# Token-major products of a hybrid decoder layer: alternating the two token tiles

## The chip, the cores and the metric

The kernel runs on one core of a Trainium2 chip. The metric is the device time of one execution in microseconds (us), lower is better. A run is an execution of the whole layer, weights read from device memory included.

## What is computed

One layer of a hybrid decoder trunk for 256 tokens and 2048 channels, all in fp32. Cut to its products:

```python
h = rms_norm(x, norm_mix_pre)
p = h @ w_in                                  # projections of three token mixers, and gate_raw
y_a, y_b, y_c = rglru(...), gated_deltanet(...), rwkv7(...)     # 1024 channels each
m = sum(sigmoid(gate_raw[b]) * (y_b @ w_branch[b]) for b in range(3))
x = x + rms_norm(m @ w_out, norm_mix_post)
h = rms_norm(x, norm_ffn_pre)
x = x + rms_norm((silu(h @ w_gate) * (h @ w_up)) @ w_down, norm_ffn_post)   # 5632 wide
```

The mixers are a gated linear recurrence, a chunked delta rule and a generalised delta rule. Nothing in the change touches their arithmetic.

## The kernel before

**Split operands.** Every large product is made from split fp32 numbers. An activation `x` is held as a high part `xh` (rounded to the type fp32r) and a low part `xl = x - xh`; a weight tile likewise as `wh` and `wl`. The product is the sum of three TensorE matmuls: `xh` with `wh` ("hi hi"), `xh` with `wl` ("hi lo"), and `xl` with `wh` ("lo hi"); the low-by-low one is left out.

**Two layouts.** `block_b` (lines 228 to 246) makes channel-major products: the weights are the stationary operand, 256 tokens move through (lines 241 to 243), into one PSUM bank. It serves the mixers' inputs. `block_a_steps` (lines 253 to 278) makes token-major products: 128 tokens of the activation are the stationary operand and 512 weight columns move through. Since there are 256 tokens, a block has two token tiles, t = 0 and t = 1, and each has an accumulator of its own, `ps[0]` and `ps[1]`, a whole PSUM bank each. The blocks are: 12 of the gates (`w_mix`, 16 channel tiles k each), 12 of the branches (`w_branch`, 8 each), 4 of `w_out` (16 each), 11 of `w_gate` and 11 of `w_up` (16 each) and 4 of `w_down` (44 each). That makes 12 x 16 + 12 x 8 + 4 x 16 + 22 x 16 + 4 x 44 = 880 steps of k, each of six matmuls: 5280.

**The change's place.** For each k, `products(t, k, h, l)` issues the three matmuls of one token tile: line 262 is hi hi, line 263 is hi lo, line 264 is lo hi. The loop calls it for tile 0 and then for tile 1:

```python
for k, h, l in self.weights(wp, src, kts, 512):
    mm = products(0, k, h, l)
    kept.append((k, h, l))
    if not last or k < kts - LATE:
        for a in kept:
            products(1, *a)
        kept = []
```

With `last` (the fourth block of `w_out` and of `w_down`) the tile 1 products of the last `LATE` = 6 steps of k are kept back and issued after all of tile 0, so that tile 0 can be emptied meanwhile.

**Weights.** `weights` (lines 190 to 218) loads 1 MB at a time into `raw` by a DMA on the queue of SyncE (SP, line 203). ScalarE (ACT) rounds 1024 columns to `wh` (line 214, three buffers), VectorE (DVE) subtracts to get `wl` (line 216, three buffers). With 512 columns one such pair serves two steps of k, which is twelve matmuls.

**Emptying.** A block's `sink` reads `ps[0]` and `ps[1]` when they are complete: the gates by ACT at line 980, the branches by DVE at lines 1058 to 1062, `w_gate` by ACT at line 1150, `w_up` by DVE at line 1154. While the mixers run, every block takes its two accumulators from a set of three banks (tag "mm"), so one of them is still being emptied when the next block begins; later, blocks take turns between two sets of three (`self.turn`).

**What sets the order.** The kernel is written with a framework that orders the instructions of each engine itself: it takes them in program order with priorities, and lets an instruction go ahead of an earlier one whose operands or buffers are, by its own model, not yet ready. So PE's order is not that of the source: a tile's first product may come later than written where its bank is not yet free, and hi lo may come later where `wl` is not yet there. Small fp32 matmuls of the mixers (and transposes, line 285) stand between the large ones, in the same queue.

**Other lines.** Line 642 and 649 (DVE) make the last result `yt` of a mixer quarter, line 650 stores it to DRAM `y` on SP's queue; line 1039 reads `y` back as `yf` for a branch, and line 1049 a kept gate. FFN block j = 0 interleaves the steps of `w_gate` and `w_up`, four of each at a time.

Of the kernel before, what the change touches and what calls it, by code (L numbers as in the profile page):

```python
# [14 lines left out]
P = 128  # L15
T = 256
D = 2048
KD = D // P
# [6 lines left out]
LATE = 6  # L25
# [115 lines left out]
class Builder:  # L141
# [108 lines left out]
        for _ in self.block_a_steps(wp, pp, src, xh, xl, kts, sink, last):  # L250
            pass

    def block_a_steps(self, wp, pp, src, xh, xl, kts, sink, last=False):
        nc = self.nc
        self.turn = 1 - getattr(self, "turn", 0)
        tag, n = ("mm", self.mm_bufs) if self.turn or self.mixers else ("ptg", self.ps_bufs["ptg"])
        ps = [pp.tile([P, 512], F32, name=self.uid("mm"), tag=tag, bufs=n) for _ in range(2)]
        kept = []

        def products(t, k, h, l):  # L260
            ts = slice(t * P, (t + 1) * P)
            nc.tensor.matmul(ps[t], xh[:, k, ts], h, start=(k == 0), stop=False)  # L262
            nc.tensor.matmul(ps[t], xh[:, k, ts], l, start=False, stop=False)  # L263
            return nc.tensor.matmul(ps[t], xl[:, k, ts], h, start=False, stop=(k == kts - 1))  # L264

        for k, h, l in self.weights(wp, src, kts, 512):
            mm = products(0, k, h, l)
            kept.append((k, h, l))
            if not last or k < kts - LATE:
                for a in kept:  # L270
                    products(1, *a)
                kept = []
            yield k
        with self.tc.issue_after(mm.ins):
            for a in kept:
                products(1, *a)
        with self.tc.high_priority(self.ahead_evac):
            sink(ps)

# [598 lines left out]
def build(tc, aps, out):  # L878
    nc = tc.nc
    b = Builder(tc)  # L880
# [5 lines left out]
    pp = b.pp = b.pool("pp", space=bass.MemoryType.PSUM)  # L886
    b.dp = b.pool("dram", space=bass.MemoryType.DRAM)
    cp = b.pool("const")
    wp = b.pool("wp")
# [3 lines left out]
    def acts(s):  # L893
        return (xp.tile([P, KD, T], F32R, name=f"{s}h", tag="xh"), xp.tile([P, KD, T], F32R, name=f"{s}l", tag="xl"))
# [6 lines left out]
    xh, xl = acts("x")  # L901
# [82 lines left out]
    def stage(s):  # L984
        return sp.tile([P, 512], F32, name=b.uid(s), tag="stage", bufs=b.stage_bufs)
# [133 lines left out]
    xh, xl = acts("h")  # L1119
    with tc.high_priority(FIRST):  # L1120
# [5 lines left out]
        last = b.to_channels(pp, group, "n3", xh, xl)  # L1126
# [18 lines left out]
    for j in range(FF // 512):  # L1145
        g = [stage("silu") for _ in range(2)]

        def gate(ps, g=g):
            for t in range(2):
                nc.scalar.activation(g[t], ps[t], AF.Silu, scale=rs[t])  # L1150

        def up(ps, g=g):
            for t in range(2):
                nc.vector.scalar_tensor_tensor(g[t], ps[t], rs[t], g[t], ALU.mult, ALU.mult)

        steps = [b.block_a_steps(wp, pp, aps[w][j], xh, xl, KD, f) for w, f in (("w_gate", gate), ("w_up", up))]
        if j == 0:
            for _ in range(0, KD, 4):
                for st in steps:
                    for _ in range(4):  # L1160
                        next(st)
        for st in steps:
            for _ in st:
                pass
        b.hold = None
        for t in range(2):
            b.split_channels(pp, g[t], ah, al, 4 * j, t)
# [49 lines left out]
```

## Time and profile before

| | |
|---|---|
| median of 3 runs | 1847.26 us (1846.95 to 1848.06) |
| the profiled execution's own time | 1846.92 us |
| its span, first to last instruction | 1845.1 us |
| PE (TensorE matmul) busy | 1827.5 us, 99% |
| PEld (weight load) busy | 1578.7 us, 86% |
| DVE busy | 1123.7 us, 61% |
| ACT busy | 863.8 us, 47% |
| mean granted TensorE clock | 0.996 of full speed |
| share of the chain that ended last | PE 96%, DVE 1%, ACT 1%, DMA 1% |

A matmul's duration in the trace runs from its start to its modelled end, and successive ones overlap; how fast the engine goes is read from the distance of their starts. In a name such as `mm<-wh,hl` the first operand is the moving one and the second the stationary one, so `wh,hl` is a weight's high part moving past an activation's low part: lo hi. Buffer numbers are left out there; which of the two accumulators a row writes is seen from the order of instructions below. `h`, `m`, `x`, `y` and `a` ahead of `h` or `l` stand for the activation: layer input `x`, mixer outputs `y`, merged `m`, FFN input `h`, FFN middle `a`.

### The profile page before, as it was taken

What the parts mean: (1) busy time and instruction counts of PE and PEld (TensorE: products, weight loads), DVE (VectorE), ACT (ScalarE), POOL (GpSimd) and SP (SyncE); (2) the same over time, 40 slices, a digit from 0 to 9 for tenths busy, and PEclk for the clock granted to TensorE, in tenths of its full rate; (3) what the DMA queues carried; (4) which work ended last, traced back from release to release, by engine and by line L of the source; (5) the groups of instructions that cost most, each with busy time, mean ns of one, the idle gap of its engine ahead of it and who ended that gap; (6) DMA issues with size and microseconds to landing.
All of it is one profiled execution on the core that took longest, in us unless ns stands there. A gap on an engine that the chain in (4) does not pass through costs nothing.

```text
span 1845.1 us, 27756 instructions
## 1 busy us (share of the span) xinstructions
PE 1827.5 (99%) x11516; PEld 1578.7 (86%) x11516; DVE 1123.7 (61%) x1652; ACT 863.8 (47%) x1089; POOL 41.0 (2%) x76
## 2 busy tenths in 40 slices
PE   9999999999999999999999999999999999999998
PEld 9999997999899988887788878888888888888886
DVE  6768567866786677746665556555545445444444
ACT  7545345534553465444444446444444444443443
POOL 0000000000100010000000000000000000000000
PEclk9999999999999999999999999999999999999999
DMA  7545445444544454657765556555555555555553
GB/s 263 176 168 183 146 148 189 168 159 138 183 170 159 144 181 161 221 179 271 279 218 185 186 202 231 197 187 185 195 191 183 187 196 187 207 203 185 202 185 136
DMA packets 58574, 347.45 MB, mean 188 GB/s; under 512 B 6480, under 2 KB 7760, under 8 KB 19920
## 3 DMA queue, kind: packets, MB, share of 16 engines
q1 hardware_dynamic: 50832, 328.23, 50.8%
q10 hardware_dynamic: 7328, 15.36, 2.3%
q8 instruction: 90, 1.47, 0.3%
q0 software_dynamic: 288, 2.10, 0.3%
q14 instruction: 36, 0.29, 0.0%
HBM read 330.98 MB, written 14.68 MB: 187 GB/s over the span
## 4 chain that ended last, share of the span: by engine, by line
PE 96%; DVE 1%; ACT 1%; DMA 1%; issue 0%; POOL 0%; ACTq 0%; POOLq 0%; DVEq 0%; SPq 0%
PE mm L263 21%; PE mm L264 21%; PE mm L262 21%; PE mm L242 8%; PE mm L241 8%; PE mm L243 8%; PE tp L285 1%; PE px L568 1%; PE pr L603 1%; PE pr L592 1%; PE psa L599 1%; DMA raw<-in_w_branch_dram 1%; PE pst L609 0%; PE px L753 0%; PE px L482 0%
## 5 line engine op out<-in xcount | busy, mean ns | idle before, releaser
L216 DVE TENSOR_TENSOR wl<-raw,wh 128x1024 fp32r<-128x1024 f32 x590 | 721.4, 1224 | 607.0 <-ACT wh L214 604.4
L214 ACT CAST wh<-raw 128x1024 fp32r<-128x1024 f32 x590 | 620.5, 1052 | 839.3 <-PE mm L264 601.8
L242 PE MATMUL mm<-xl,wh 128*128 128x256 f32 x1200 | 342.5, 286 | 1.6 <-DVE xl L915 1.5
L241 PE MATMUL mm<-xh,wh 128*128 128x256 f32 x1200 | 342.8, 286 | 0.1
L243 PE MATMUL mm<-xh,wl 128*128 128x256 f32 x1200 | 341.4, 285 | 0.0
L264 PE MATMUL mm<-wh,hl 128*128 128x512 f32 x704 | 274.7, 390 | 0.0
L263 PE MATMUL mm<-wl,hh 128*128 128x512 f32 x704 | 274.6, 390 | 0.0
L262 PE MATMUL mm<-wh,hh 128*128 128x512 f32 x704 | 250.9, 392 | 2.0 <-ACT hh L311 2.0
L242 PEld LDWEIGHTS mm<-xl,wh 128*128 128x128 f32 x1200 | 229.8, 191 | 3.6 <-DVE xl L915 2.2
L241 PEld LDWEIGHTS mm<-xh,wh 128*128 128x128 f32 x1200 | 229.8, 191 | 1.9 <-ACT xh L914 0.5
L243 PEld LDWEIGHTS mm<-xh,wl 128*128 128x128 f32 x1200 | 229.5, 191 | 0.9 <-issue 0.3
L262 PEld LDWEIGHTS mm<-wh,hh 128*128 128x128 f32 x704 | 132.4, 188 | 29.6 <-ACT hh L311 2.6
L263 PEld LDWEIGHTS mm<-wl,hh 128*128 128x128 f32 x704 | 132.5, 188 | 27.6 <-DVE wl L216 0.4
L264 PEld LDWEIGHTS mm<-wh,hl 128*128 128x128 f32 x704 | 132.4, 188 | 27.5
L263 PE MATMUL mm<-wl,xh 128*128 128x512 f32 x384 | 151.7, 395 | 0.3 <-DVE wl L216 0.3
L264 PE MATMUL mm<-wh,xl 128*128 128x512 f32 x384 | 150.6, 392 | 0.0
L262 PE MATMUL mm<-wh,xh 128*128 128x512 f32 x384 | 141.3, 392 | 0.0
L264 PE MATMUL mm<-wh,al 128*128 128x512 f32 x352 | 136.9, 389 | 0.0
L263 PE MATMUL mm<-wl,ah 128*128 128x512 f32 x352 | 136.9, 389 | 0.0
L262 PE MATMUL mm<-wh,ah 128*128 128x512 f32 x352 | 123.6, 389 | 0.0
L263 PEld LDWEIGHTS mm<-wl,xh 128*128 128x128 f32 x384 | 72.1, 188 | 16.9 <-issue 1.0
L262 PEld LDWEIGHTS mm<-wh,xh 128*128 128x128 f32 x384 | 72.1, 188 | 16.0 <-issue 1.3
(297 smaller groups left out, 1951.4 us busy)
## 6 DMA issues: line engine op xcount, KB each, us to landing
raw<-in_w_in_dram SPq DMA_DIRECT2D x72, 1024.0 KB, 4.9
raw<-in_w_mix_dram SPq DMA_DIRECT2D x48, 1024.0 KB, 5.0
raw<-in_w_gate_dram SPq DMA_DIRECT2D x44, 1024.0 KB, 4.8
raw<-in_w_up_dram SPq DMA_DIRECT2D x44, 1024.0 KB, 4.9
raw<-in_w_down_dram SPq DMA_DIRECT2D x44, 1024.0 KB, 4.9
raw<-in_w_branch_dram SPq DMA_DIRECT2D x24, 1024.0 KB, 4.9
raw<-in_w_out_dram SPq DMA_DIRECT2D x16, 1024.0 KB, 4.8
keep<-stage ACTq DMA_DIRECT2D x28, 256.0 KB, 4.4
```

Of the source, the lines that this page charges most:

```text
L214: nc.scalar.copy(wh[:, :n], s)
L216: nc.vector.tensor_tensor(wl[:, :n], s, wh[:, :n].bitcast(F32), ALU.subtract)
L241: nc.tensor.matmul(o, hs, xh[:, k], start=(k == 0 and c == 0), stop=False, skip_group_check=True)
L242: nc.tensor.matmul(o, hs, xl[:, k], start=False, stop=False, skip_group_check=True)
L243: nc.tensor.matmul(o, ls, xh[:, k], start=False, stop=(k == kts - 1), skip_group_check=True)
L262: nc.tensor.matmul(ps[t], xh[:, k, ts], h, start=(k == 0), stop=False)
L263: nc.tensor.matmul(ps[t], xh[:, k, ts], l, start=False, stop=False)
L264: return nc.tensor.matmul(ps[t], xl[:, k, ts], h, start=False, stop=(k == kts - 1))
L285: nc.tensor.transpose(ps[:, k], src[:, k * P:(k + 1) * P], self.cst("id"))
L568: nc.tensor.matmul(ps[h][:, n * P:(n + 1) * P], bkc[hs, c, n], arc[hs, c, n], start=True, stop=True)
L592: nc.tensor.matmul(pq[bb, us], st[u][:, n, bb], sav[:, n, us], start=not n, stop=True, skip_group_check=True)
L599: nc.tensor.matmul(ps[bb, us], X[bb, 2 * u + p], R[bb, us], start=True, stop=True)
```

## The change

`products` now takes a list of token tiles. For each of the three kinds (hi hi, hi lo, lo hi) it issues that kind for every tile of the list, so that with both tiles listed each matmul adds to the other bank than the one before it. The order of the three kinds within a tile is the same as before. FFN block j = 0 passes `paired=False`, which keeps the old order tile by tile, and the kept-back steps of a `last` block are still issued one tile after the other. Matmuls, weight loads, loads, casts and evictions are the same in number and size.

```diff
--- before.py
+++ after.py
@@ -250,30 +250,31 @@
         for _ in self.block_a_steps(wp, pp, src, xh, xl, kts, sink, last):
             pass
 
-    def block_a_steps(self, wp, pp, src, xh, xl, kts, sink, last=False):
+    def block_a_steps(self, wp, pp, src, xh, xl, kts, sink, last=False, paired=True):
         nc = self.nc
         self.turn = 1 - getattr(self, "turn", 0)
         tag, n = ("mm", self.mm_bufs) if self.turn or self.mixers else ("ptg", self.ps_bufs["ptg"])
         ps = [pp.tile([P, 512], F32, name=self.uid("mm"), tag=tag, bufs=n) for _ in range(2)]
         kept = []
 
-        def products(t, k, h, l):
-            ts = slice(t * P, (t + 1) * P)
-            nc.tensor.matmul(ps[t], xh[:, k, ts], h, start=(k == 0), stop=False)
-            nc.tensor.matmul(ps[t], xh[:, k, ts], l, start=False, stop=False)
-            return nc.tensor.matmul(ps[t], xl[:, k, ts], h, start=False, stop=(k == kts - 1))
+        def products(ts, k, h, l):
+            for a, w, first, end in ((xh, h, True, False), (xh, l, False, False), (xl, h, False, True)):
+                for t in ts:
+                    mm = nc.tensor.matmul(ps[t], a[:, k, t * P:(t + 1) * P], w, start=first and k == 0,
+                                          stop=end and k == kts - 1)
+            return mm
 
         for k, h, l in self.weights(wp, src, kts, 512):
-            mm = products(0, k, h, l)
-            kept.append((k, h, l))
-            if not last or k < kts - LATE:
-                for a in kept:
-                    products(1, *a)
-                kept = []
+            if last and k >= kts - LATE:
+                mm = products((0,), k, h, l)
+                kept.append((k, h, l))
+            else:
+                for ts in ((0, 1),) if paired else ((0,), (1,)):
+                    mm = products(ts, k, h, l)
             yield k
         with self.tc.issue_after(mm.ins):
             for a in kept:
-                products(1, *a)
+                products((1,), *a)
         with self.tc.high_priority(self.ahead_evac):
             sink(ps)
 
@@ -1153,7 +1154,7 @@
             for t in range(2):
                 nc.vector.scalar_tensor_tensor(g[t], ps[t], rs[t], g[t], ALU.mult, ALU.mult)
 
-        steps = [b.block_a_steps(wp, pp, aps[w][j], xh, xl, KD, f) for w, f in (("w_gate", gate), ("w_up", up))]
+        steps = [b.block_a_steps(wp, pp, aps[w][j], xh, xl, KD, f, paired=j > 0) for w, f in (("w_gate", gate), ("w_up", up))]
         if j == 0:
             for _ in range(0, KD, 4):
                 for st in steps:
```

All products of `block_a_steps` now have line 263, and lines below it have numbers one higher than before.

**First place: PE, start of a `w_gate` block of the FFN (j = 3).** `mm_11988` is the accumulator of tile 0, `mm_11989` that of tile 1; `wh_11992` and `wl_11993` are the first 1024 split weight columns. Before:

```order
L262 MATMUL mm_11988<-wh_11992,hh 128x512
L262 MATMUL mm_11989<-wh_11992,hh 128x512
L263 MATMUL mm_11988<-wl_11993,hh 128x512
L264 MATMUL mm_11988<-wh_11992,hl 128x512
L263 MATMUL mm_11989<-wl_11993,hh 128x512
L264 MATMUL mm_11989<-wh_11992,hl 128x512
L262 MATMUL mm_11988<-wh_11992,hh 128x512
L263 MATMUL mm_11988<-wl_11993,hh 128x512
L264 MATMUL mm_11988<-wh_11992,hl 128x512
L262 MATMUL mm_11989<-wh_11992,hh 128x512
L263 MATMUL mm_11989<-wl_11993,hh 128x512
L264 MATMUL mm_11989<-wh_11992,hl 128x512
```

and now:

```order
L263 MATMUL mm_11988<-wh_11992,hh 128x512
L263 MATMUL mm_11989<-wh_11992,hh 128x512
L263 MATMUL mm_11988<-wl_11993,hh 128x512
L263 MATMUL mm_11989<-wl_11993,hh 128x512
L263 MATMUL mm_11988<-wh_11992,hl 128x512
L263 MATMUL mm_11989<-wh_11992,hl 128x512
L263 MATMUL mm_11988<-wh_11992,hh 128x512
L263 MATMUL mm_11989<-wh_11992,hh 128x512
L263 MATMUL mm_11988<-wl_11993,hh 128x512
L263 MATMUL mm_11989<-wl_11993,hh 128x512
L263 MATMUL mm_11988<-wh_11992,hl 128x512
L263 MATMUL mm_11989<-wh_11992,hl 128x512
```

The twelve matmuls of a pair of k steps are the same. Before, six of the twelve steps from one to the next (with that into the following group) change the accumulator and six do not; now all twelve change it. The first hi hi of tile 1 already stood second before.

**Second place: PE, end of gate block 8 and start of gate block 9 in the mixers' stage.** `mm_8764` and `mm_8765` are tiles 0 and 1 of the ending block, `mm_8909` and `mm_8910` those of the next, which share a set of three banks. Before (the last product of `mm_8764` stands three rows above the first of these):

```order
L781 MATMUL px_8116<-XT_8102,U_7428 64x64 x4
L264 MATMUL mm_8765<-wh_8886,xl 128x512
L262 MATMUL mm_8909<-wh_8913,xh 128x512
L263 MATMUL mm_8909<-wl_8914,xh 128x512
L264 MATMUL mm_8909<-wh_8913,xl 128x512
L262 MATMUL mm_8909<-wh_8913,xh 128x512
L263 MATMUL mm_8909<-wl_8914,xh 128x512
L264 MATMUL mm_8909<-wh_8913,xl 128x512
L262 MATMUL mm_8909<-wh_8929,xh 128x512
L603 MATMUL pr_7908<-sav_6817,st_6840 64x64 x4
L609 MATMUL pst_7926<-sav_6817,bkt_6827 128x128 x2
L262 MATMUL mm_8910<-wh_8913,xh 128x512
```

and now (the first product of `mm_8910` stands three rows of `mm_8909` behind these):

```order
L263 MATMUL mm_8765<-wl_8887,xh 128x512
L263 MATMUL mm_8764<-wh_8886,xl 128x512
L263 MATMUL mm_8765<-wh_8886,xl 128x512
L263 MATMUL mm_8909<-wh_8913,xh 128x512
L263 MATMUL mm_8909<-wl_8914,xh 128x512
L263 MATMUL mm_8909<-wh_8913,xl 128x512
L263 MATMUL mm_8909<-wh_8913,xh 128x512
L263 MATMUL mm_8909<-wl_8914,xh 128x512
L263 MATMUL mm_8909<-wh_8913,xl 128x512
L263 MATMUL mm_8909<-wh_8929,xh 128x512
L600 MATMUL psa_7941<-R_7939,X_7885 64x64 x4
L802 MATMUL px_8142<-ut_8135,kd_7449 128x128 x2
```

Tile 0 of the ending block now gets its last product one matmul before the block's end rather than three. The next block begins with products of its tile 0 alone, seven of them before and ten now, until tile 1 begins. The small fp32 matmuls between them are others than before. Over the whole program PE's stream has 160 groups of small matmuls between the large ones, before and now; of the 5279 steps from one token-major matmul to the next, 2920 stay on the same accumulator before and 514 now.

**Third place: SP's queue, where the second branch begins.** `raw` is a load of 1 MB of weights, `y_113<-yt` the store of the last quarter of the third mixer's result, `gate` a kept gate. Before:

```order
L1049 DMA gate_9218<-keep_6091 128x512
L1049 DMA gate_9293<-keep_6236 128x512
L203 DMA raw_9387<-in_w_branch_dram 128x2048
L650 DMA y_113<-yt_8023 128x512
L203 DMA raw_9421<-in_w_branch_dram 128x2048
L1049 DMA gate_9294<-keep_6236 128x512
L1049 DMA gate_9381<-keep_8181 128x512
```

and now:

```order
L1050 DMA gate_9218<-keep_6091 128x512
L1050 DMA gate_9293<-keep_6236 128x512
L651 DMA y_113<-yt_8023 128x512
L203 DMA raw_9387<-in_w_branch_dram 128x2048
L203 DMA raw_9421<-in_w_branch_dram 128x2048
L1050 DMA gate_9294<-keep_6236 128x512
L1050 DMA gate_9381<-keep_8181 128x512
```

The store, which waits for DVE's `yt`, stood behind the load of `raw_9387` and now stands ahead of it. From `raw_9421` on SP's order is as before.

## Rows read from the trace of the kernel before

**Rows 1.** The page's head and part 1: busy us, share of span, instructions.

```profile
span 1845.1 us, 27756 instructions
...
PE 1827.5 (99%) x11516; PEld 1578.7 (86%) x11516; DVE 1123.7 (61%) x1652; ACT 863.8 (47%) x1089; POOL 41.0 (2%) x76
```

**Rows 2.** Busy time by stretch; columns: stretch, length, engines' busy (x), PEclk, DMA share, GB/s.

```profile
281.00:470.00 189.00, 189.00 (x1665) 172.95 (x1664) 136.94 (x265) 93.36 (x129) 9.02 (x14) 1.00 0.48 163
870.00:930.00 60.00, 59.00 (x258) 47.87 (x257) 41.43 (x45) 25.03 (x25) 0.00 (x0) 1.00 0.80 287
1640.00:1834.00 194.00, 194.00 (x857) 160.64 (x856) 90.45 (x79) 78.32 (x84) 0.21 (x1) 1.00 0.51 179
```

**Rows 3.** Groups by line and form: busy us, mean ns | idle before.

```profile
L216 DVE TENSOR_TENSOR wl<-raw,wh 128x1024 fp32r<-128x1024 f32 x590 | 721.4, 1224 | 607.0 <-ACT wh L214 604.4
...
L262 PE MATMUL mm<-wh,hh 128*128 128x512 f32 x704 | 250.9, 392 | 2.0 <-ACT hh L311 2.0
```

**Rows 4.** Timeline of PE in `w_down`: start us, us, what, count [idle before].

```profile
1700.04 0.62 PE L262 MATMUL mm<-wh,ah 128*128 128x512 f32 x2
1700.50 0.39 PE L263 MATMUL mm<-wl,ah 128*128 128x512 f32 x1
...
1702.76 0.62 PE L262 MATMUL mm<-wh,ah 128*128 128x512 f32 x2
...
1825.16 0.61 PE L262 MATMUL mm<-wh,ah 128*128 128x512 f32 x2
```

**Rows 5.** Timeline of PE, first and last of the 36 products ending `w_down` tile by tile.

```profile
1827.88 0.39 PE L262 MATMUL mm<-wh,ah 128*128 128x512 f32 x1
...
1835.82 0.39 PE L264 MATMUL mm<-wh,al 128*128 128x512 f32 x1
```

**Rows 6.** Timeline of PE, channel-major products of 256 columns, nine steps apart.

```profile
579.02 0.28 PE L242 MATMUL mm<-xl,wh 128*128 128x256 f32 x1
...
580.10 0.28 PE L242 MATMUL mm<-xl,wh 128*128 128x256 f32 x1
```

**Rows 7.** Timeline of PE: its longest waits between token-major products before 930 us.

```profile
737.85 0.50 PE L263 MATMUL mm<-wl,xh 128*128 128x512 f32 x1 [0.34 <-DVE wl L216]
...
880.57 0.50 PE L262 MATMUL mm<-wh,yh 128*128 128x512 f32 x1 [0.73 <-ACT yh L1041]
...
882.02 0.73 PE L264 MATMUL mm<-wh,yl 128*128 128x512 f32 x2 [0.25 <-DVE yl L1042]
```

**Rows 8.** Timelines of PE and ACT at the end of gate block 8.

```profile
788.89 0.40 PE L264 MATMUL mm<-wh,xl 128*128 128x512 f32 x1
...
789.33 0.69 ACT L980 ACTIVATE stage<-mm,rstd 128x512 f32<-128x512 f32 x1 [0.46 <-PE mm L264]
```

**Rows 9.** Timelines of SP, DVE, ACT, PE, and the `raw` tile's landing times, 845 to 885 us.

```profile
856.13 0.33 SPq L203 DMA_DIRECT2D raw<-in_w_branch_dram  x1
...
859.56 0.32 SPq L650 DMA_DIRECT2D y<-yt  x1
...
858.84 0.69 DVE L649 TENSOR_TENSOR yt<-yt,px 128x512 f32<-128x512 f32 x1
...
869.00 1.06 ACT L214 CAST wh<-raw 128x1024 fp32r<-128x1024 f32 x1 [0.26 <-PE mm L264]
...
871.52 0.84 PE L262 MATMUL mm<-wh,yh 128*128 128x512 f32 x3
...
DMA to landing us min/median/max: 4.7/7.1/9.7
```

**Rows 10.** A stretch at the lower clock: columns as in rows 2; and one product in it.

```profile
1101.40:1108.00 6.60, 5.61 (x17) 3.50 (x16) 6.60 (x14) 3.32 (x12) 0.00 (x0) 0.50 0.48 201
...
1107.07 0.63 PE L263 MATMUL mm<-wl,hh 128*128 128x512 f32 x1
1107.49 0.63 PE L264 MATMUL mm<-wh,hl 128*128 128x512 f32 x1
```

## The prediction

> **What bounds the kernel now.** I read the page's head first, then the busy times by stretch, then PE's timeline in the places that the change rewrites. PE is busy in 99% of the span [rows 1]. That alone does not say that PE is at its pace, because successive matmuls overlap; so the stretches come next. In a mixer quarter PE is busy in all of 189.00 us, in `w_down` in all of 194.00 us at a granted clock of 1.00, and even where the branches wait for their inputs only 1.00 us of 60 is idle [rows 2]. No other engine comes near. So the time is the number of PE's matmuls times the distance between their starts, plus the few places where PE waits. The change leaves the number alone, so it has to act on the distance or on the waits.
>
> The number of token-major matmuls is 5280, from the loops; the group of FFN inputs shows its share, 704 hi hi = 22 blocks x 16 k x 2 tiles [rows 3]. Their distance is read from `w_down`: from the start at 1700.04 to that at 1825.16 lie 46 groups of twelve (1700.04 to 1702.76 is one), so 552 steps in 125.12 us, 226.7 ns each [rows 4]. 5280 x 226.7 ns = 1197 us, about two thirds of the span. That is what the change can touch.
>
> **The change part by part.**
>
> *Which accumulator the next matmul adds to.* The order at the first place shows that before the change half of the steps already go to the other accumulator, in the sequence 0 1 0 0 1 1 0 0 0 1 1 1. The trace of before therefore prices both kinds of step. In the timeline the pair of hi hi (0 then 1) together with the step back to 0 takes 1700.50 - 1700.04 = 0.46 us, two changing steps of 0.23 [rows 4]. A sharper comparison is with the end of `w_down`, where 36 products run tile by tile: 35 steps, 34 of them staying, take 1835.82 - 1827.88 = 7.94 us, 226.9 ns each, give or take 0.3 for the rounding of the rows [rows 5]. The mean of half and half is 226.7 [rows 4], so a changing step is at most 2 x 0.2 = 0.4 ns shorter than a staying one, with an uncertainty of 0.6. By the orders, 2920 - 514 = 2406 steps turn from staying to changing. 2406 x 0.4 ns = 1.0 us, with bounds from a loss of 0.5 us to a gain of 2.4 us. I take zero, since the difference is inside the rounding, and keep both ends.
>
> There is a fixed part in the distance that one could hope to remove. The channel-major matmuls, half as wide, are 1.08 us / 9 = 120 ns apart [rows 6]; so 256 more columns cost 106.7 ns, and 226.7 - 2 x 106.7 = 13.3 ns are paid per matmul whatever its width. This part is there in changing steps as well as in staying ones, by the comparison just made. [...]
>
> *The order hi hi, hi lo, lo hi across tiles.* It asks for `wl` after two matmuls instead of one. At the first place the order before had tile 1's hi hi second too, so nothing changes there. Zero.
>
> *Emptying at a block's end.* Tile 0 gets its last product one matmul before the end rather than three, so its emptying starts 2 x 0.227 = 0.45 us later. It is covered if the bank is free before the next block's tile 1 wants it. At the second place the last product of tile 0 started at 788.89, and ACT's read began at 789.33 and took 0.69 [rows 8]: the bank is free 1.13 us after that start, 5 matmuls. If ACT has a cast of 1.06 us in front [rows 9], it is 2.19 us, under 10 matmuls. The new order puts the rest of the old block (one) and ten of the new block's tile 0 there, besides small matmuls: 11 x 0.227 = 2.5 us. Covered, zero; without that cover each end would cost up to 0.45 us. After the mixers a block takes its banks from the other set and has a whole block's time.
>
> *The rest of PE's stream.* The groups of small matmuls are 160 before and now, so switching between kinds of matmul costs the same. But in the mixers other small matmuls stand at other points, and what they wait for is reshuffled. What there is to win is small: the longest waits between token-major products before 930 us are 0.34 + 0.73 + 0.25 = 1.3 us as shown idle [rows 7]; adding the part that the overlap hides (each such row's matmul starts at most 0.16 us past its predecessor's normal step before idleness shows) gives about 1.8 us. What there is to lose I bound by the same rows twice over, 3.5 us. I take zero here, because nothing in the order favours a sign.
>
> *SP's queue.* At the third place the store of `yt` is moved ahead of a 1 MB load. Before, that load was issued at 856.13 and the store at 859.56, when DVE's last step on `yt` (858.84 + 0.69 = 859.53) was done [rows 9]. Now the load waits for the store: it goes out at about 859.56 + 0.32 = 859.9, or 3.75 us later. It lands 4.7 to 9.7 us after issue, so by 869.6 at the latest. ACT's cast of its first half was at 869.00, released by PE and not by the load, and PE's first product with it at 871.98 (the third of the row of three) [rows 9]. A cast begun at 869.6 ends at 870.66, and DVE's subtraction of 1.22 us [rows 3] at 871.9. Hidden, by 0.1 us at the worst landing and 5 us at the best. Loads behind it wait for `raw` buffers, as before.
>
> *The sum.* 1846.92 (the profiled execution, span 1845.1 and 1.8 around it) + 0 + 0 + 0 + 0 + 0. That execution is 0.3 us below the median of the runs, 1847.26, so for the median I forecast **1847.2 us**: no change. About 0.2% (3.7 us) is what a measurement of this kernel can tell from no change. The ends of the unknown terms, added, are a gain of 2.4 + 1.8 = 4.2 and a loss of 0.5 + 3.5 = 4.0; as they will hardly all fall together, the range takes about 3 us either way.
>
> **The rivals.**
>
> *The bank's turnaround is real but hidden in the rows.* If long alternation removed the 13.3 ns where two alternating steps did not, 2406 x 13.3 ns = 32 us would go: 1815 us. Against it: 552 half-alternating steps and 35 staying ones have the same distance to 0.4 ns. For it: no run of more than five alternations stands in the old order. That the change does not alternate is no rival: by the new order 4765 of 5279 steps do, and those that still stay are where a bank is not yet free. Chance 0.03.
>
> *Reshuffled waits in the mixers* (faster side). All of the 4.2 us above: 1843. Chance 0.02.
>
> *SP's queue turns into PE's wait* (slower side). If DVE finishes `yt` later in the new order, the store holds the weight load for as long, and each us past the slack is a us of PE, in a stretch where DMA is already at a share of 0.80 [rows 2]. With `yt` 5 us later and the landing at its worst, PE would wait 5 us: 1852. It decides from 0.1 us of delay at the slow landing, from 5 us at the fast one. For it: PE was held by late inputs 9 us further on [rows 7]. Chance 0.04, other lost waits of the reshuffle included.
>
> *The emptying is not covered.* Of the gates 10 blocks, of the branches 8 share the three banks; at their 18 ends 0.45 us each come to 8 us: 1855. Against it: the slack of 2.5 against 1.1 to 2.2 us. Chance 0.02.
>
> *The clock falls.* If going from bank to bank made PE pause so that its clock dropped, each product would cost what it does in the one stretch at 0.50 of the clock, 1107.49 - 1107.07 = 0.42 us [rows 10], 0.2 us more; one product in a hundred so would be 53 x 0.2 = 11 us, 1858. That stretch came after PE had waited for transposes, not in a stream of products; in `w_down`, half alternating, the clock is 1.00 [rows 2]. [...] Chance 0.01.
>
> **How the numbers follow.** The forecast has 0.88. Faster by over 0.2%: 0.03 + 0.02 = 0.05. Slower: 0.04 + 0.02 + 0.01 = 0.07. The range 1844.3 to 1850.3 leaves out the rivals and little else.
>
> **What would show it.** In the profile after, 552 steps of `w_down` should again take 125.1 us with every step changing the accumulator; the channel-major step should still be 120 ns; PE should be busy 1.00 of `w_down` and of the FFN. The load of `raw_9387` should go out right behind the store near 859.9 and PE should not wait for it. A distance below 226 ns, or a quarter of the mixers a few us longer than 189, would prove the forecast wrong, the first in its main step, the second in the reshuffle.

## The result, and the profile after

The changed kernel takes 1858.25 us (median of 4 runs, 1857.76 to 1862.49) against 1847.11 us: 1.0065 times the time before, 95% interval 1.0053 to 1.0077. It is **slower by about 11 us**, where no change was forecast. The profiled execution took 1857.76 us. Its page begins so (columns as in [rows 1]):

```profile
span 1856.0 us, 27748 instructions
...
PE 1831.5 (99%) x11516; PEld 1582.5 (85%) x11516; DVE 1122.7 (60%) x1652; ACT 859.3 (46%) x1088; POOL 41.5 (2%) x76
```

The span is 10.9 us longer than in [rows 1], and PE has the same number of matmuls. Is the step longer? `w_down` in the changed kernel, in PE's timeline, 46 groups of twelve apart as in [rows 4]:

```profile
1710.92 0.61 PE L263 MATMUL mm<-wh,ah 128*128 128x512 f32 x2
1711.37 0.62 PE L263 MATMUL mm<-wl,ah 128*128 128x512 f32 x2
...
1836.04 0.61 PE L263 MATMUL mm<-wh,ah 128*128 128x512 f32 x2
```

The difference of the starts is 125.12 us, to the last digit that of [rows 4], now with every step going to the other accumulator. In `w_down` alternating is worth nothing, neither way. Busy time by stretch (columns as in [rows 2]), first the changed kernel:

```profile
281.00:850.00 569.00, 560.88 (x4529) 492.79 (x4527) 392.66 (x757) 278.17 (x386) 21.81 (x31) 0.99 0.49 168
...
870.00:930.00 60.00, 60.00 (x267) 49.56 (x266) 39.41 (x42) 25.82 (x26) 0.00 (x0) 1.00 0.85 312
1640.00:1834.00 194.00, 194.00 (x857) 160.64 (x856) 90.88 (x77) 78.91 (x84) 0.00 (x0) 1.00 0.54 190
```

and the kernel before in the mixers:

```profile
281.00:850.00 569.00, 568.66 (x4579) 499.18 (x4578) 403.25 (x769) 286.22 (x394) 23.96 (x32) 1.00 0.51 173
```

Between 281 and 850 us PE now stands idle for 8.12 us instead of 0.34, and makes 50 matmuls fewer. In the branches it has gained the 1.00 us that [rows 2] showed idle; `w_down` is unchanged. So the loss is in the mixers. What PE waits for there, as the list of waits has it (engine, operation and line that waited, what released it: us in total, times, longest):

```profile
PE px L422 <- issue: 2.5, 1, 2.5
PE mm L263 <- DVE wl L216: 1.9, 1, 1.9
PE mm L243 <- DVE wl L216: 1.3, 1, 1.3
PE px L483 <- DMA upt<-in_up_dram: 0.9, 1, 0.9
PE mm L241 <- ACT wh L214: 0.8, 1, 0.8
PE mm L263 <- ACT stage L981: 0.7, 1, 0.7
```

In the kernel before the same list has one entry, 0.3 us ([rows 7], the first). Two kinds of new wait make up most of the sum.

**Split weights that come late.** One wait is for a `wh`, ACT's cast of a weight tile, 0.8 us; two are for a `wl`, DVE's subtraction, 1.3 + 1.9 us. DVE's timeline shows what stands in front of a subtraction. Before, in the first quarter after the gate blocks begin:

```profile
348.54 3.35 DVE L866 RECIPROCAL rec<-rec 128x512 f32<-128x512 f32 x1
351.92 0.35 DVE L396 SCALAR_TENSOR_TENSOR sv<-st,cst_t,sv 32x128 f32<-32x128 f32 x1
352.31 1.23 DVE L216 TENSOR_TENSOR wl<-raw,wh 128x1024 fp32r<-128x1024 f32 x1
```

and in the changed kernel, with ACT's next cast and PE's wait for it:

```profile
352.87 3.35 DVE L867 RECIPROCAL rec<-rec 128x512 f32<-128x512 f32 x1
356.13 1.16 DVE L216 TENSOR_TENSOR wl<-raw,wh 128x1024 fp32r<-128x1024 f32 x1
...
356.71 1.04 ACT L214 CAST wh<-raw 128x1024 fp32r<-128x1024 f32 x1 [1.83 <-PE mm L242]
...
357.81 0.39 PE L241 MATMUL mm<-xh,wh 128*128 128x256 f32 x1 [0.78 <-ACT wh L214]
```

The RECIPROCAL of the gated linear recurrence holds DVE for 3.35 us. In the changed kernel it runs 4.3 us later against the products, and in both kernels a subtraction is done only behind it. The wait for `wh` at 357.81 us does not come out of that, though. The cast at 356.71 us began as the product that freed its buffer ended (356.39 + 0.28 us), and up to then PE had not stopped; the cast took 1.04 us, and PE's order wants its result before it is done. In the two waits for `wl` the RECIPROCAL does stand in the chain, for instance in the third quarter (DVE's and PE's timelines of the changed kernel):

```profile
730.30 3.34 DVE L867 RECIPROCAL rec<-rec 128x512 f32<-128x512 f32 x1
...
733.97 2.34 DVE L216 TENSOR_TENSOR wl<-raw,wh 128x1024 fp32r<-128x1024 f32 x2
...
735.23 0.50 PE L263 MATMUL mm<-wl,xh 128*128 128x512 f32 x1 [1.86 <-DVE wl L216]
```

The first of these two subtractions ends at 735.18 us, and PE goes on at 735.23. The wait at 548.05 us stands in the same way behind the RECIPROCAL at 543.33.

**A wait without a releaser, and the half clock after it.** The longest wait is put down to "issue". PE's timeline, then two stretches (columns as in [rows 2]), all of the changed kernel:

```profile
393.01 0.53 PE L422 MATMUL px<-D,W 32*32 32x32 f32 x18 [2.54 <-issue]
```

```profile
379.20:390.50 11.30, 11.27 (x252) 10.85 (x251) 7.93 (x16) 3.15 (x3) 0.00 (x0) 1.00 0.53 187
392.70:399.50 6.80, 6.49 (x75) 6.21 (x77) 2.35 (x5) 1.05 (x1) 0.00 (x0) 0.51 0.14 27
```

PE stopped within a group of 96 small matmuls. After it the granted clock was 0.51 for 6.8 us, and 75 matmuls were made where the kernel before makes 99 in the same stretch at 1.00. What PE may have lacked is seen in the DMA queues (packets, MB, share of 16 engines), first on the page, for the whole span:

```profile
q8 instruction: 90, 1.47, 0.3%
```

and then by stretch: 379.2 to 380.3 us, 380.6 to 390.5 us (where q8 has no row, nor has it between 380.3 and 380.6), 390.5 to 391.8 us.

```profile
q8 instruction: 1, 0.02, 5.5%
...
q1 hardware_dynamic: 286, 2.10, 60.3%
...
q8 instruction: 1, 0.02, 4.6%
```

The page calls queue q8 "instruction" and gives it 90 packets in all, 1.47 MB / 90 = 16 KB each; 11516 matmuls with as many weight loads, over 90, are 256 instructions to a packet. So its packets are taken here for blocks of PE's code, an estimate from these counts. One came at 379.2 us; until 390.5 no other came, while PE made 252 matmuls and 251 weight loads, about two blocks' worth. The 2.10 MB of queue q1 are two loads; the second of them, issued at 386.00 us (`raw_648`), was on its way until the block began at 390.62 us, as that load's last packet ended. The block had landed at 391.57 us, and PE went on at 393.01.

So the theory before the experiments was this: alternating is free; by moving PE's products it shifted the mixers' other work, and this put (D) the RECIPROCAL in front of the making of `wh` and `wl` and (F) a code block's fetch behind a weight load in a group of small matmuls, where PE goes through code fastest (78 matmuls in 0.87 us from 389.61 us on).

### The profile page after: what moved, and what is told of

Read it like the earlier page. It is cut to its first block, busy times and chain, and to the rows that moved or that the text cites. A ratio compares the mean times of both kernels' runs of the same rounds, so it can differ in the third digit from the quotient of the medians.

```text
span 1856.0 us, 27748 instructions
## 1 busy us (share of the span) xinstructions
PE 1831.5 (99%) x11516; PEld 1582.5 (85%) x11516; DVE 1122.7 (60%) x1652; ACT 859.3 (46%) x1088; POOL 41.5 (2%) x76
## 3 DMA queue, kind: packets, MB, share of 16 engines
q8 instruction: 90, 1.47, 0.3%
## 4 chain that ended last, share of the span: by engine, by line
PE 96%; DVE 1%; ACT 1%; DMA 1%; issue 1%; POOL 0%; ACTq 0%; POOLq 0%; DVEq 0%; SPq 0%
PE mm L263 64%; PE mm L242 8%; PE mm L243 8%; PE mm L241 8%; PE tp L286 1%; PE px L569 1%; PE pr L604 1%; PE pr L593 1%; PE psa L600 1%; PE pst L610 0%; PE px L754 0%; PE px L483 0%; DMA upt<-in_up_dram 0%; PE px L720 0%; DVE x L1124 0%
## 5 line engine op out<-in xcount | busy, mean ns | idle before, releaser
L263 PE MATMUL mm<-wh,hl 128*128 128x512 f32 x704 | 223.6, 391 | 0.0
L263 PE MATMUL mm<-wl,hh 128*128 128x512 f32 x704 | 223.3, 391 | 0.0
L263 PE MATMUL mm<-wh,hh 128*128 128x512 f32 x704 | 220.6, 390 | 2.0 <-ACT hh L312 2.0
L263 PE MATMUL mm<-wl,xh 128*128 128x512 f32 x384 | 125.4, 396 | 1.9 <-DVE wl L216 1.9
L263 PE MATMUL mm<-wh,xh 128*128 128x512 f32 x384 | 124.8, 393 | 0.7 <-ACT stage L981 0.7
L263 PE MATMUL mm<-wh,xl 128*128 128x512 f32 x384 | 123.9, 391 | 0.0
L263 PE MATMUL mm<-wh,al 128*128 128x512 f32 x352 | 109.4, 389 | 0.0
L263 PE MATMUL mm<-wl,ah 128*128 128x512 f32 x352 | 109.4, 389 | 0.0
L263 PE MATMUL mm<-wh,ah 128*128 128x512 f32 x352 | 109.3, 389 | 0.0
```

What stands on the lines that cost most here:

```text
L263: mm = nc.tensor.matmul(ps[t], a[:, k, t * P:(t + 1) * P], w, start=first and k == 0, stop=end and k == kts - 1)
```

## Experiments

The runs of the kernel before lay between 1847.0 and 1847.6 us (medians) in every comparison.

**Where the loss is (e1, e2).** e1 alternates only after the mixers, e2 only in them.

```diff
+        paired = paired and not self.mixers
...
+        paired = paired and self.mixers
```

(The first line is e1, the second e2.)

> The tiles alternate only in the products after the mixers; in the mixers the products go tile by tile, as in the kernel before. Theory S (the step from product to product costs 226.7 ns in either order, and the whole loss of some 11 us is made in the mixers, by the order of the other work there): within 1 us of the kernel before, 1846 to 1848 us, and no stretch at clock 0.50 near 393 us. Theory B (changing banks costs something at each product): the loss goes with the number of alternating products, most of which lie after the mixers, so 1852 us or more.

> The reverse: the tiles alternate only in the mixers, and go tile by tile after them. Theory S: the whole loss stays, 1857 to 1859 us. Theory B: a smaller part of the loss stays, 1853 us or less.

e1: 1847.84 us, ratio 1.0001 (0.9991 to 1.0010), and its only wait in the mixers is the 0.34 us of [rows 7]. e2: 1857.52 us, 1.0055 (1.0040 to 1.0070), with all six waits of the changed kernel, for instance:

```profile
393.08 0.37 PE L423 MATMUL px<-D,W 32*32 32x32 f32 x18 [2.56 <-issue]
```

Theory S holds: of the 880 steps of k only those in the mixers matter (10 gate blocks and 8 branch blocks, 224 steps), and no loss per matmul shows.

**Half loads (e3).** Each load of 1 MB is cut into two DMAs.

```diff
-            n = gk // 2 if self.feeds else gk
+            n = gk // 2
```

> The changed kernel with each load of 1 MB of weights cut into two DMAs of half the size, nothing else. Theory F (PE stood still for 2.54 us before 393.01 because its next instructions were fetched by the DMA engines behind a weight load, and the clock fell after it): the fetch gets through between the halves, the wait is under 1 us, the clock holds 0.97 or more from 392 to 400 us, and 4 to 6 us of the 11 come back, 1852 to 1854 us. Rival D (only the work of DVE and ACT in front of weight casts counts, and the fetch was late for another reason): the wait and the half clock stay, 1857 to 1859 us, or more if the longer queue of issues on SP costs something.

1860.04 us, 1.0071 (1.0054 to 1.0088). A miss: the wait stayed.

```profile
390.76 2.58 issue
```

This row is of its chain of waits. The halves followed each other closely: in the seven slices of 0.625 us from 386.9 to 391.3 us the DMA engines moved 59 to 393 GB/s, and none was empty. So no gap for a code block shows, and the run decides nothing about theory F.

**LRU written first (e4).**

```diff
-        b.solve16(C, xc, [sv[:, i] for i in range(2, 5)])
         lru(q)
+        b.solve16(C, xc, [sv[:, i] for i in range(2, 5)])
```

> The changed kernel with the elementwise work of the LRU written ahead of the solve in each quarter, so that in the first quarter DVE's RECIPROCAL of 3.3 us no longer stands between the solve's steps and a weight subtraction; PE's order is that of the changed kernel. Theory D (DVE's order makes the waits): the wait of 1.06 us at 356.75 goes, and with it the shift that brings PE's small matmuls against the weight load near 390 us; 1852 to 1856 us. Theory F alone: the wait before 393 us stays, and the time is 1856 to 1859 us.

1858.01 us, 1.0059 (1.0044 to 1.0074). The edit did not do what it was made for. The RECIPROCAL began only 0.43 us earlier, in the same gap of DVE, and the subtraction still came behind it:

```profile
352.44 3.35 DVE L867 RECIPROCAL rec<-rec 128x512 f32<-128x512 f32 x1
355.70 0.63 DVE L342 TENSOR_TENSOR slab<-mm,rbc 128x512 f32<-128x512 f32 x1
...
356.47 1.22 DVE L216 TENSOR_TENSOR wl<-raw,wh 128x1024 fp32r<-128x1024 f32 x1
```

All waits stayed. The subtraction behind the RECIPROCAL began 0.34 us later than in the changed kernel and PE's wait for `wh` kept its 0.78 us, so that wait does not go with it. About the waits for `wl` the run tells nothing.

**The code shifted (e5).**

```diff
+        for _ in range(51):
+            self.nc.tensor.matmul(ps[0:32, 0:32], self.rst128[0:32, 0:32], self.rst128[0:32, 0:32], start=True, stop=True)
...
-        b.warm_up(pp, 13)
+        b.warm_up(pp, 10)
```

> The changed kernel with 48 more small matmuls in the warm-up at the start (51 of 32x32, and 10 instead of 13 of 128x128), which shifts all later code of PE by 96 matmul records against the blocks of 128 records in which it is fetched; PE's order from the first quarter to the fourth is that of the changed kernel. Theory F (the block of code that PE needed in its burst of small matmuls fell due while a load of 1 MB was in progress, and came only after it): the block is now due some 4 us earlier, before the load; the wait of 2.54 us before 393 goes, the clock holds 0.97 or more from 392 to 400 us, and 5 to 6 us come back: 1851 to 1854 us, give or take 1 us for the start. Rival (the wait is made by something in the program at that point, a semaphore or a bank): it stays in its place, 1857 to 1859 us.

1855.81 us, 1.0047 (1.0030 to 1.0064). The wait before 393 us is gone and the clock is 1.00 (busy time by stretch):

```profile
392.00:400.00 8.00, 8.00 (x195) 7.47 (x183) 4.28 (x9) 3.34 (x6) 0.00 (x0) 1.00 0.40 136
```

Of the five other waits that for `upt` is gone too; the four others are in their places, for instance (PE's timeline):

```profile
359.89 0.39 PE L243 MATMUL mm<-xh,wh 128*128 128x256 f32 x1 [0.78 <-ACT wh L214]
544.73 0.39 PE L245 MATMUL mm<-xh,wl 128*128 128x256 f32 x1 [1.33 <-DVE wl L216]
```

The start cost 359.89 - 357.81 = 2.1 us, and between these two waits 548.05 - 544.73 + 2.1 = 5.4 us came back. PE's order is here that of the changed kernel up to 759 us, so no semaphore or bank made the wait: what the edit moved was the place of the code in its blocks. One of them now came at 382.5 us, ahead of the next load's packets, which began at 383.2. The total fell by 2.4 instead of the 4 to 7 expected: the start took 2.1, and from 664.3 to 667.7 us PE was at half its pace again (products of 256 columns 0.21 us apart instead of 0.12; the clock over 660 to 850 us was 0.99).

**The load itself (e13).** Of one load, the one issued at 386.00 us, an eighth is brought; the order of every engine is that of the changed kernel.

```diff
-                        self.load = nc.sync.dma_start(rv[:, i:i + n], src[k0 // g][:, i:i + n]).ins
+                        self.load = nc.sync.dma_start(rv[:, i:i + part], src[k0 // g][:, i:i + part]).ins
...
+                if part == 1 and not self.feeds:
+                    s = rv[:, 0:1].to_broadcast([P, hk, width])
```

> The changed kernel with one single load cut: that of the weight tile raw_648, issued at 386.00 us, brings 128 KB (one k of 256 columns) instead of 1 MB, and its casts read those columns eight times over (so the rest of that tile's weights is left out). The order on every engine is that of the changed kernel. Theory F' (the code block came late because that load's packets were ahead of it): the wait of 2.54 us before 393 us and the half clock after it are gone, nothing else changes, and 5 to 6 us come back, 1852 to 1853.5 us; the waits at 357.8, 548, 665, 730 and 735 stay or shift by the same amount. Rival (the block is late for a reason of its own, such as when it was asked for): the wait stays above 2 us and the time at 1857 to 1859 us.

In its timeline the group of 96 runs through, in its list of waits the entry for "issue" is gone and the five others stay, and the stretch after is at full clock:

```profile
358.21 0.38 PE L247 MATMUL mm<-xh,wh 128*128 128x256 f32 x1 [0.78 <-ACT wh L220]
...
390.00 1.27 PE L428 MATMUL px<-D,W 32*32 32x32 f32 x96
...
543.27 0.39 PE L249 MATMUL mm<-xh,wl 128*128 128x256 f32 x1 [1.35 <-DVE wl L222]
```

```profile
392.70:399.50 6.80, 6.80 (x126) 6.22 (x127) 2.98 (x4) 3.54 (x8) 0.00 (x0) 1.00 0.44 157
```

Between the waits at 358 and 543 us, 548.05 - 543.27 + (358.21 - 357.81) = 5.2 us came back: 2.5 of the wait and, as an estimate, the other 2.7 of the clock, 1.00 instead of 0.51 over these 6.8 us. A block of q8 came at 388.6 us, behind the small load and ahead of the group of 96. The load was the cause. The total, 1855.74 us (1852.79 to 1857.24; 1.0046, 1.0029 to 1.0063), returned less than the 5 to 6 us expected. In the profiled execution the wait at 735.23 comes only 3.15 us earlier (732.08), so 548.05 - 543.27 - 3.15 = 1.6 us are lost again in between, behind the wait for `upt`:

```profile
660.78 1.10 PE L489 MATMUL px<-los,upt 64*128 64x256 f32 x4 [1.00 <-DMA upt<-in_up_dram]
```

```profile
663.00:666.40 3.40, 3.40 (x15) 3.23 (x16) 1.60 (x4) 0.87 (x1) 1.63 (x1) 0.52 0.88 255
```

The changed kernel has nearly the same wait (0.93 us at 665.49) without that stretch. In e2 and e3, with the changed kernel's waits, the clock was 0.76 from 393 to 400 us, where the changed kernel's was 0.55, and 0.99 from 660 to 850 us, where the changed kernel's was 1.00; in e2 products of 256 columns start 0.21 us apart instead of 0.12 from 667.39 us on. Why it fell at one place or the other stays open.

**Is it alternating, or where things fall? (e6, e7).** e6 takes tile 1 first for each kind; e7 leaves the first two gate blocks in the old order.

```diff
-                for t in ts:
+                for t in reversed(ts):
...
+        self.nblk = getattr(self, 'nblk', 0) + 1
+        paired = paired and (not self.mixers or self.nblk > 2)
```

(The first two lines are e6, the last two e7.)

> The changed kernel with the two tiles alternating in the other sequence, tile 1 ahead of tile 0 for each kind. The number of alternating steps is the same. Theory S (the loss is in how the other work of the mixers happens to fall, not in alternating): the waits of the mixers lie elsewhere and sum to another number, so a time more than 2 us away from the changed kernel's 1858, most likely between 1846 and 1855 us. Rival I (alternating costs the mixers something by itself, since both accumulators are completed together and emptied late): 1856 to 1860 us, with the waits on the emptying.

> The changed kernel, but the first two gate blocks, which fill the second quarter's start, go tile by tile as before; the other 18 blocks of the mixers alternate. Theory S: with the first quarter as before, the wait at 356 us, that before 393 us and the half clock after it are gone; of the loss of 11 us some 6.5 come back, 1850 to 1853 us, unless the later waits move too. Rival I: 18 of 20 alternating blocks keep 9/10 of the loss, 1856 to 1858 us.

e6: 1849.27 us, 1.0012 (1.0003 to 1.0021), though it alternates as much as the changed kernel. e7: 1852.29 us, 1.0026 (1.0014 to 1.0038), with 16 of the mixers' 18 blocks alternating (the expectation had counted them as 20). Both as theory S expected, and in both the waits lie elsewhere. The first two rows are of e6, whose profiled execution was the slowest of its ten (1851.97 us):

```profile
391.58 0.45 PE L422 MATMUL px<-D,W 32*32 32x32 f32 x30 [0.65 <-issue]
583.24 0.52 PE L422 MATMUL px<-D,W 32*32 32x32 f32 x36 [2.13 <-issue]
```

and these of e7:

```profile
547.12 0.39 PE L241 MATMUL mm<-xh,wh 128*128 128x256 f32 x1 [0.78 <-ACT wh L214]
582.07 0.39 PE L424 MATMUL px<-D,W 32*32 32x32 f32 x24 [2.34 <-issue]
```

With the first quarter as before, e7 has neither wait of that quarter. A wait without a releaser, the 2.34 us above, stands in the next quarter's group of small matmuls instead.

**The RECIPROCAL (e8, e11, e12).** e8 cuts it into four of 128 columns; e11 (changed kernel) and e12 (kernel before) leave it out.

```diff
-        nc.vector.reciprocal(rec, rec)
+        for i in range(4):
+            nc.vector.reciprocal(rec[:, i * P:(i + 1) * P], rec[:, i * P:(i + 1) * P])
```

(The added lines are of e8 alone.)

> The changed kernel with the LRU's RECIPROCAL of 3.35 us on DVE cut into four of 128 columns. Theory D (weight subtractions wait behind it, and PE behind them): PE's waits at 356.75 (1.06 us) and at 732.98 (2.25 us) shrink below 0.5 us each, 2 to 3 us come back, 1854 to 1856 us; if the earlier PE also moves the burst away from the load near 390 us, 1849 to 1851 us. Rival: the waits stay within 0.3 us, and the time with them, 1857 to 1859 us.

> The changed kernel without the RECIPROCAL of the LRU (4 of 3.35 us on DVE; it leaves that operation out, so the LRU's values differ). Theory D (what the casts waited for is the RECIPROCAL, set among the solve's steps): PE's waits for wh or wl at 357.8, 548.1, 729.9 and 735.2, 4.6 us idle in all, go to below 1 us in all; with the late code block still there 1852 to 1854 us, without it (PE's order moves) 1847 to 1849 us. Rival (something else, as the solve's steps themselves, makes the casts late): these waits stay above 3 us in all.

> The kernel before without the RECIPROCAL, the control of e11. Theory D: in the kernel before the RECIPROCAL ran where nothing waited for it, so there is nothing to gain: 1846 to 1848 us. Rival: if leaving DVE work out is itself worth something, below 1845 us, and e11's gain is to be read against it. A late code block near a burst of small matmuls would add 2 to 6 us here too.

e8: 1854.14 us, 1.0038 (1.0023 to 1.0053). The waits at 735, for `upt` and for `stage` are gone, those at 358 and 547 stay, three of 0.4 to 0.8 us are new, and the wait without a releaser near 390 us is still there, 2.05 us. PE's order differs from the changed kernel's from 573 us on, so the wait at 735 decides nothing. Cutting did not let a subtraction in between; the four ran in one go, and the subtraction came behind the last:

```profile
353.06 3.38 DVE L868 RECIPROCAL rec<-rec 128x128 f32<-128x128 f32 x4
356.36 1.16 DVE L216 TENSOR_TENSOR wl<-raw,wh 128x1024 fp32r<-128x1024 f32 x1
```

e11: 1847.89 us, 1.0005 (0.9996 to 1.0014). None of the changed kernel's waits for `wh` or `wl` is left. This is what D expects; but PE's order moved too, the wait without a releaser near 390 us went with it, and another took its place (1.12 us at 748.80, its only wait in the mixers), so e11 alone does not prove D. e12, its control, missed its 1846 to 1848 us: 1850.68 us, 1.0018 (1.0009 to 1.0027), **slower** with less work. In the kernel before, too, the mixers' order moved. A wait without a releaser came, as the expectation's last sentence allowed, and with it a wait for `wh`:

```profile
380.80 0.73 PE L421 MATMUL px<-D,W 32*32 32x32 f32 x62 [1.05 <-issue]
...
468.08 0.50 PE L262 MATMUL mm<-wh,xh 128*128 128x512 f32 x1 [0.78 <-ACT wh L214]
```

This program has no RECIPROCAL, and its wait is as long as that for `wh` in the changed kernel, e2 to e5, e7, e8 and e13. So a wait for `wh` needs no RECIPROCAL, and with the timeline and e4 theory D does not hold for it; whether the RECIPROCAL had a part in it by way of the scheduler, which set PE's order, is open. For the two waits for `wl` theory D rests on the timelines: no run took the RECIPROCAL out and left PE's order as it was.

**The code shift on both sides (e9, e10).** The shift of e5 on e6 and on the kernel before.

> The kernel of e6 (tile 1 first) with the code shift of e5 (51 matmuls of 32x32 and 10 instead of 13 of 128x128 in the warm-up); PE's order in the mixers is that of e6. In e6 two waits of 0.65 and 2.13 us stood in the bursts of small matmuls near 391 and 583 us, and a short stretch at half clock after the second. Theory F: both go, 3 to 4.5 us come back, and the start costs the 2 us that it costs in e10: within 1 us of e10, so alternating all 20 blocks of the mixers costs nothing that can be measured. Rival (alternating costs the mixers something by itself): the time stays at least 2 us above e10.

> The kernel before with the same code shift. It prices the shift itself: e5 began its mixers some 2 us later. Theory F and its rivals: 1848.5 to 1850 us, no waits over 1 us in the mixers, unless a burst of the kernel before now meets a load, which would show as a wait without a releaser of 2 to 2.6 us near 390, 581 or 770 us and add 2 to 6 us.

e10: 1849.85 us, 1.0018 (1.0009 to 1.0027), as expected: the start's price, no new wait. e9: 1851.48 us, 1.0025 (1.0016 to 1.0034), 1.6 us above e10, between the two expectations. Of e6's two waits without a releaser one is gone and one is shorter:

```profile
583.75 0.25 PE L424 MATMUL px<-D,W 32*32 32x32 f32 x4 [0.86 <-issue]
```

In the profiled executions, 1850.34 against 1849.72, e9 is 0.6 us above e10 with this wait of 0.86 us and no other over 0.35 in the mixers. But e10 also waits 0.72 and 0.26 us in the branches, for `yh` and `yl`, which e9 does not. Ahead of the branches e9 is 1.9 us behind (its last channel-major product starts at 659.83 us, e10's at 657.88), and that wait is about half of it. So these runs do not show that alternating costs the mixers nothing: about 1 us was not traced.

## Why the prediction was wrong

- **The step between products** was the main term, and it was right: 226.7 ns before and after, 125.12 us for 552 steps, and e1 at 1.0001. The 13.3 ns stayed when every step changed the accumulator, so no run shows a turnaround of the bank in them.
- **The order of kinds, and SP's queue**: zero was right. The load behind the store went out at 870.34 us, not near 859.9, because the mixers ended later, and PE did not wait for it. The branches are even 1.0 us faster, without PE's wait there.
- **The emptying** was put at zero for all 18 ends. One shows, 0.67 us for ACT's `stage` at 729.90. The rival with 8 us was wrong.
- **The rest of PE's stream** is the step that failed: "What there is to lose I bound by the same rows twice over, 3.5 us." It measured 10.9. The late code block makes 5.2 of it (by the stretch between two waits in e13's trace; e13's median fell by 2.5). The three waits for `wh` and `wl` are 0.78 + 1.34 + 1.86 = 4.0 us as shown idle, the other two 0.93 + 0.67 = 1.6; with the 0.16 us that overlap hides in each of five, 0.8 more. The branches give 1.0 back: 5.2 + 4.0 + 1.6 + 0.8 - 1.0 = 10.6, which leaves 0.3 open; PE's wait among the FFN's transposes, 1.00 us at 1114.23 against 0.51 before, is not in it, so the sum is good to about half a us. The 5.2 are shown by e13, the rest is read from the timelines.
- The bound failed for two reasons. It took the waits that the kernel before happened to have as a measure of those that a new order can have; but that order was nearly free of waits, with 0.34 us idle in 569, so a change of it could hardly do anything but lose. And it had no term for the code's fetch, since the trace of before shows no such wait; its page does show queue q8 and the groups of small matmuls.
- **The clock** fell, but not as the rival had it. It followed a wait of 2.54 us, not the alternation, and stayed down for 6.8 us, not for one product in a hundred. That this rival's 1858 us is the time measured is luck.
- The sentence "a quarter of the mixers a few us longer than 189, would prove the forecast wrong, [...] in the reshuffle" named what came.

None of the versions run beats the kernel before. With 0.34 us idle in the mixers, 1.00 in the branches [rows 2] and a step of 226.7 ns in both orders, there was about 1.3 us to find in the mixers and the branches.

## What to carry to other kernels

In a program whose engines' orders are set by a scheduler, an edit that is worth zero where it acts still draws a new order for everything around it; e1, e6, e7 and the changed kernel, which differ only in where and in which sequence they alternate, lie between 1847.8 and 1858.3 us. Where the old order has almost no idle time, bound that draw by what can newly come to stand in front of a product, not by the waits of the old trace, and give the loss the larger chance. Here that was up to 1.9 us behind the RECIPROCAL, 0.8 us for a cast, and 5.2 us for a late code block with the half clock after it. No run tried such a bound as a forecast. Put an edit with no gain of its own only where the order is insensitive to it (e1), or leave it.

## What the runs showed of the hardware

- PE stood still until code came. In the changed kernel no block of q8 came from 380.3 to 390.5 us; one began at 390.62 us, as the last packet of a load of 1 MB ended, and had landed at 391.57. PE stood for 2.54 us and went on at 393.01 us, 1.44 us after the landing. Groups of 96 small matmuls took 1.02 us (e7, 391.37 us) to 1.27 us (e13, 390.00 us), so 128 matmuls with their weight loads, the 256 instructions of a block, last 1.4 to 1.7 us at that pace, an estimate from these two times. The runs have eleven waits without a releaser in the mixers, of 0.65 us (e6) to 2.58 us (e3); the block and the load are shown here for that of the changed kernel alone. Cutting the load in halves left the wait (2.58 us in e3); moving the code (e5) or shrinking the load to an eighth (e13) took it away.
- The kernel before passed this place with little to spare: its block landed at 390.65 us, and PE came to its 3415th matmul, the count at which the changed kernel stopped, at 391.91 us, 1.26 us later, less than the 1.44 us that PE took in the changed kernel. The old trace shows no wait there, but hardly any slack either.
- What follows such a wait differs. After 2.54 us in the changed kernel the clock was 0.51 for 6.8 us; after 2.56 us in e2 it was 0.76 from 393 to 400 us; e7's wait of 2.34 us was followed by a clock of 1.00:

```profile
582.00:586.00 4.00, 3.93 (x89) 3.76 (x90) 1.99 (x4) 1.05 (x1) 0.00 (x0) 1.00 0.02 4
```

- A RECIPROCAL of 512 columns took 3.35 us on DVE in the kernel before and in the changed one, nearly three times the subtraction of 1024 columns (1.22 us, [rows 3]), and cut in four it took 3.38 (e8).
